# Delta rule inversion: 64x64 products paired across quarters of the array, four steps in place of five

## The chip, the cores and the metric

The kernel runs on one core of a Trainium2 chip. The metric is the device time of one execution in microseconds (us). A core has a matrix engine (TensorE, PE in the profile, with its weight loads listed as PEld), a vector engine (VectorE, DVE), a scalar engine (ScalarE, ACT), GpSimd (POOL) and SyncE (SP), which issues most DMAs. Each engine works through its own instructions in order and waits for others on semaphores. TensorE writes to PSUM; a PSUM tile must be read out (evacuated) by another engine before its buffer can be written again.

## The reference, cut to what matters

The program is one step of a two-layer encoder: a gated DeltaNet layer, then a layer of sliding-window attention. It works on 2048 prompt tokens and 32 sample tokens, with 8 heads of width 128. The delta rule is evaluated in blocks. For each block and head a lower triangular matrix with ones on its diagonal is built from the keys, and two right-hand sides are solved with it:

```python
lower = jnp.where(strict, jnp.einsum('nbhik,nbhjk->nbhij', kbeta, kc) * decay, 0.0)
tmat = lower + jnp.eye(c, dtype=lower.dtype)
u = lax.linalg.triangular_solve(tmat, vc * bc[..., None], left_side=True, lower=True, unit_diagonal=True)
...
def step(s, xs):
    v_new = ui - jnp.einsum('bhck,bhkv->bhcv', wi, s)
    o = jnp.einsum('bhck,bhkv->bhcv', qd, s) + jnp.einsum('bhij,bhjv->bhiv', ai, v_new)
    s = s * gl[..., None, None] + jnp.einsum('bhck,bhcv->bhkv', kd, v_new)
```

The state `s` goes from block to block, so the blocks follow one another.

## The kernel before

The kernel has stages. First come the projections of the DeltaNet layer with its convolution (class `P1`), then the delta rule (class `Delta`), then the layer's output projection with its norm (`O1`), the projections of the second layer (`P2`) and the attention (`Attention`). All products are in 32-bit floats, and one product appears in the profile as two passes of weight load and matmul.

The delta rule takes 17 chunks: the 32 sample tokens, and 16 chunks of 128 prompt tokens. The 16 big chunks need an inverse of a 128x128 unit triangular matrix for each of 8 heads. It is built up in sizes. The inverses of the 32x32 diagonal blocks come from an elimination on GpSimd and VectorE (`chain`, L546), and are transposed into place on VectorE and ScalarE (`spread`, L622, with the results `tcf` and `u32`). The method `invert` (L637) combines them on TensorE, for all 8 heads at a time. It is a generator: each `yield` ends a step, and the loop in `run` decides by its order of `next` calls what stands between the steps. `npr` holds the matrix, `u` the transposed inverse, and "lo" and "hi" below are rows or columns 0-63 and 64-127. The steps are:

1. `y1p` (L653): 32x32 products; ScalarE writes them, negated, into `y1` (L655).
2. `tp` (L659): 8 products from rows lo to columns lo; ScalarE copies them to `ta` lo (L661).
3. `up` (L666): 16 products, for each head one lo to lo and one hi to hi; two copies into `u` (L667, L668).
4. `y2p` (L672): 8 products, rows lo to columns hi; a copy to `ta` hi (L673).
5. `u2p` (L677): 8 products, rows hi to columns lo; ScalarE writes them, negated, into `u` (L678).

The PSUM tiles come from pools: `pa` (two buffers, shared with the transposes `tr` and `vtr` and the products `g` and `gq` of neighbouring chunks) and `pb` (one buffer). The steps use `pb`, `pa`, `pb`, `pa`, `pb`, in this order.

`run` (L775) works on several chunks at once. In pass `i` it finishes the recurrence for chunk `i`, inverts for chunk `i+1`, prepares chunk `i+2` and loads for chunk `i+3`. The orders of TensorE, VectorE and ScalarE are those of the program text (a manual schedule), so an instruction that waits holds back all that stands behind it on its engine. In one pass the calls around the inversion are, in order: step 1; step 2 among small VectorE operations; the transpose of keys `tr` (`turn_k`, L569) with its evacuation into `kd` by ScalarE (L572); steps 3 and 4; the transpose of values `vtr` (L583) with its evacuation into `vn` (L588); the exponentials `gb` (L611); the first product of `seen` (L712); the second `tr` and `kd`; the decays `E` (L518); step 5. The next pass begins with `lower` (L522) for another chunk, whose two groups of products `g` (L533) are read by VectorE into `npr` (L534). Then comes `changes` (L691): the products `vp` (L698) of `u` and `vn`, copied to `vs` by ScalarE (L700). From `vs` follow the outputs, the new state on VectorE (L734) and the next `errors` (`ks`, L687).

Between these, a `Filler` puts independent projection products (L77 to L79, tile `ps`) into TensorE's order in the first eleven passes, in fixed amounts; at the end products of the output projection (L1089 to L1091, tile `po`) take their place.

## Time and profile before

| | |
|---|---|
| median of 3 runs | 2277.91 us (2274.84 to 2278.19) |
| span of the profiled execution | 2272.4 us |
| TensorE (PE) busy | 2192.9 us (97%) |
| VectorE (DVE) busy | 1376.3 us (61%) |
| ScalarE (ACT) busy | 898.1 us (40%) |
| GpSimd (POOL) busy | 829.3 us (36%) |
| first step 1 to last step 5 of the inversions | 761.2 to 1183.6 us |

The profiled execution's own time is not listed beside its span; the span runs from its first to its last instruction, and lies 2.4 to 5.8 us below the runs' times, which take in what is around it. A row in order of time has the start and the length in us, the engine, the line, the operation, the tile written and the tiles read, the shapes, and a count of merged instructions; in brackets stand the idle time of the engine before it and what ended it. A row by line has counts and durations in ns, and below it who waited, as us and times. PE spans are modelled and overlap, since matmuls are pipelined. PEclk is the granted TensorE clock in tenths of full speed.

### The profile page before, as it was taken

The page shows a single profiled execution, that of the slowest core. Times are in us where ns is not written, and L with a number is a line of the kernel's source. Part 1 is how long each engine was busy: PE and PEld are TensorE (multiplying, and loading weights), DVE is VectorE, ACT ScalarE, POOL GpSimd, SP SyncE. Part 2 cuts the span into 40 slices and gives each one's busy share as a digit, 9 for nine tenths or more (in the row PEclk, how much of TensorE's full clock was granted, in tenths as well). Part 3 has the DMA queues.
Part 4 walks back from the last instruction along what each step waited for, and adds up shares of the span by engine and source line. Part 5 has one row for each costly group of instructions (what it writes and reads, how often), then busy time and mean ns, then how long its engine had stood idle before and what let it go on. Part 6 is the DMA issues. An engine that isn't in the chain of part 4 may idle for free.

```text
span 2272.4 us, 36806 instructions
## 1 busy us (share of the span) xinstructions
PE 2192.9 (97%) x13810; PEld 2008.0 (88%) x13810; DVE 1376.3 (61%) x2709; ACT 898.1 (40%) x2230; POOL 829.3 (36%) x1185
## 2 busy tenths in 40 slices
PE   8999999999998999999999999999999999999997
PEld 6999999999997888898888787999999987778884
DVE  3766666744385677777768875224443235668774
ACT  4444444333233566666642212311111235535541
POOL 1412121212120577766720201323442124556563
PEclk9999999999999999999889999999999999999998
DMA  5121212232435455557736764742212277233311
GB/s 191 66 77 66 75 66 80 103 108 103 126 114 144 93 129 130 120 125 186 189 91 196 227 192 149 252 146 70 73 68 77 83 179 249 75 94 96 109 61 51
DMA packets 282722, 274.49 MB, mean 121 GB/s; under 512 B 68608, under 2 KB 247104, under 8 KB 279200
## 3 DMA queue, kind: packets, MB, share of 16 engines
q1 hardware_dynamic: 270544, 248.84, 38.0%
q10 hardware_dynamic: 12000, 23.30, 2.9%
q8 instruction: 109, 1.79, 0.3%
q14 instruction: 69, 0.57, 0.1%
HBM read 168.53 MB, written 103.92 MB: 120 GB/s over the span
## 4 chain that ended last, share of the span: by engine, by line
PE 84%; ACT 6%; DMA 4%; DVE 3%; issue 1%; SPq 1%; POOL 0%; ACTq 0%; DVEq 0%; POOLq 0%
PE ps L77 16%; PE ps L79 16%; PE ps L78 16%; PE ot L1510 4%; PE po L1395 2%; PE po L1089 2%; PE po L1397 2%; PE po L1396 2%; PE po L1091 2%; PE po L1090 2%; PE S L1489 2%; PE tr L1504 2%; PE vp L698 2%; ACT kd L572 1%; DMA v<-s_v 1%
## 5 line engine op out<-in xcount | busy, mean ns | idle before, releaser
L77 PE MATMUL ps<-act_hi,w_hi 128*128 128x416 f32 x2000 | 707.9, 355 | 14.3 <-DVE z L266 7.9
L79 PE MATMUL ps<-act_hi,w_lo 128*128 128x416 f32 x2000 | 705.7, 353 | 2.8 <-DVE w_lo L54 1.8
L78 PE MATMUL ps<-act_lo,w_hi 128*128 128x416 f32 x2000 | 702.3, 351 | 0.0
L77 PEld LDWEIGHTS ps<-act_hi,w_hi 128*128 128x128 f32 x2000 | 377.6, 189 | 19.4 <-issue 8.6
L79 PEld LDWEIGHTS ps<-act_hi,w_lo 128*128 128x128 f32 x2000 | 376.5, 188 | 7.9 <-DVE w_lo L54 3.1
L78 PEld LDWEIGHTS ps<-act_lo,w_hi 128*128 128x128 f32 x2000 | 377.1, 189 | 4.5 <-DVE act_lo L69 0.2
L54 POOL TENSOR_TENSOR w_lo<-w_raw,w_hi 128x1024 fp32r<-128x1024 f32 x51 | 134.5, 2638 | 559.5 <-ACT w_hi L53 541.7
L196 DVE SCALAR_TENSOR_TENSOR y<-R,convw,y 128x2083 f32<-128x2083 f32 x72 | 173.7, 2414 | 110.1 <-POOL convo L190 56.9
L556 POOL TENSOR_TENSOR tm<-L,Tt 128x60 f32<-128x60 f32 (+19 forms) x373 | 140.0, 375 | 138.3 <-DVE tm L556 57.3
L1497 POOL TENSOR_TENSOR P<-P,sm 128x384 f32<-128x384 f32 (+2 forms) x128 | 100.5, 806 | 179.4 <-DVE sm L1374 104.3
L559 POOL TENSOR_TENSOR Tt<-Tt,tm 128x60 f32<-128x60 f32 (+19 forms) x373 | 151.7, 407 | 29.2
L1370 ACT ACTIVATE P<-S,nm 128x192 f32<-128x192 f32 (+2 forms) x260 | 104.7, 419 | 93.3 <-DVE nm L1363 40.4
L226 ACT COPY R<-ps 128x416 f32<-128x416 f32 (+1 forms) x144 | 61.2, 448 | 202.3 <-PE ps L79 177.7
L53 ACT CAST w_hi<-w_raw 128x1024 fp32r<-128x1024 f32 x62 | 65.0, 1048 | 146.2 <-PE ps L78 110.4
L1089 PE MATMUL po<-wo_hi,g_hi 128*128 128x512 f32 (+1 forms) x272 | 111.0, 408 | 2.9 <-ACT hT L1142 1.8
L1232 POOL TENSOR_TENSOR rs<-rs,sin 128x416 f32<-128x416 f32 x50 | 71.0, 1420 | 116.0 <-DVE rs L1231 102.1
L1091 PE MATMUL po<-wo_hi,g_lo 128*128 128x512 f32 (+1 forms) x272 | 107.3, 395 | 0.0
L1090 PE MATMUL po<-wo_lo,g_hi 128*128 128x512 f32 (+1 forms) x272 | 107.2, 394 | 0.0
L1510 PE MATMUL ot<-pt,vd 128*128 128x256 f32 x372 | 98.7, 392 | 2.1 <-ACT pt L1506 1.6
L1395 PE MATMUL po<-wo,g_hi 128*128 128x512 f32 x240 | 99.3, 414 | 0.0
L1397 PE MATMUL po<-wo,g_lo 128*128 128x512 f32 x240 | 96.2, 401 | 0.0
L1396 PE MATMUL po<-wo,g_hi 128*128 128x512 f32 x240 | 96.1, 400 | 0.0
(284 smaller groups left out, 4021.4 us busy)
## 6 DMA issues: line engine op xcount, KB each, us to landing
w_raw<-in_w_in SPq DMA_DIRECT2D x40, 512.0 KB
w_raw<-in_b_w_in SPq DMA_DIRECT2D x20, 512.0 KB
gb<-s_gcum SPq DMA_DIRECT2D x34, 256.0 KB
k<-s_k SPq DMA_DIRECT2D x34, 256.0 KB
s_z<-z SPq DMA_DIRECT2D x40, 208.0 KB
s_bz<-za SPq DMA_DIRECT2D x40, 208.0 KB
s_bq<-ra SPq DMA_DIRECT2D x40, 208.0 KB
s_q<-y SPq DMA_DIRECT2D x8, 1024.0 KB
```

The costliest lines, as they stand in the source:

```text
L77: nc.tensor.matmul(ps, hi[:, k, :], xh[:, k, :], start=(k == 0), stop=False)
L78: nc.tensor.matmul(ps, hi[:, k, :], xl[:, k, :], start=False, stop=False)
L79: nc.tensor.matmul(ps, lo[:, k, :], xh[:, k, :], start=False, stop=(k == KC - 1))
L196: nc.vector.scalar_tensor_tensor(out=y[:], in0=R[:, j:j + W], scalar=self.convw[:, i, j:j + 1], in1=y[:], op0=ALU.mult, op1=ALU.add)
L559: P.tensor_tensor(out=Tt[:n, i0:, :w], in0=Tt[:n, i0:, :w], in1=tm[:n, i0 - k:, :w], op=ALU.subtract)
L1089: nc.tensor.matmul(ps[:n], ghi[:, k, :n], w[0][:, k, cs], start=(k == 0), stop=False)
L1090: nc.tensor.matmul(ps[:n], ghi[:, k, :n], w[1][:, k, cs], start=False, stop=False)
L1091: nc.tensor.matmul(ps[:n], glo[:, k, :n], w[0][:, k, cs], start=False, stop=(k == KC - 1))
L1395: nc.tensor.matmul(ps[:n], ghi[:, k, :n], w[0][:, k, cs], start=(k == 0), stop=False)
L1396: nc.tensor.matmul(ps[:n], ghi[:, k, :n], w[1][:, k, cs], start=False, stop=False)
L1397: nc.tensor.matmul(ps[:n], glo[:, k, :n], w[0][:, k, cs], start=False, stop=(k == KC - 1))
L1510: nc.tensor.matmul(ot[:, p], self.vd[:, kc0 + j, p, :], pt[:, 2 * j:2 * j + 2, :], start=(j == 0), stop=(j == nj - 1))
```

## The change

Steps 2 to 4 become two. The product for `u` hi moves from step 3 up to step 2, and the product `y2p` moves from step 4 up to step 3. In the loops the two kinds of products alternate, so that neighbours use different quarters of the array. The copies on ScalarE move with them; their number stays. The last step's tile comes from `pa` instead of `pb`, by the alternation of the pools. `run` calls one step less after the side work.

```diff
+        lo, hi = halves
         tp = new(self.pa)
         for p in range(8):
-            nc.tensor.matmul(tp[:64, p, :], u32[:64, p, :], y1[:64, p, :], start=True, stop=True)
+            nc.tensor.matmul(tp[lo, p, :], u32[lo, p, :], y1[lo, p, :], start=True, stop=True)
+            nc.tensor.matmul(tp[hi, p, :], y1[hi, p, :], u32[hi, p, :], start=True, stop=True)
         ta = sml.tile([128, 8, 64], F32, tag="ta", name="ta")
-        nc.scalar.copy(ta[:64], tp[:64])
+        nc.scalar.copy(ta[lo], tp[lo])
+        nc.scalar.copy(u[hi, :, 64:128], tp[hi])
         yield
-        up = new(self.pb)
+        yp = new(self.pb)
         for p in range(8):
-            for hv in halves:
-                nc.tensor.matmul(up[hv, p, :], y1[hv, p, :], u32[hv, p, :], start=True, stop=True)
-        nc.scalar.copy(u[0:64, :, 0:64], up[0:64])
-        nc.scalar.copy(u[64:128, :, 64:128], up[64:128])
+            nc.tensor.matmul(yp[lo, p, :], y1[lo, p, :], u32[lo, p, :], start=True, stop=True)
+            nc.tensor.matmul(yp[hi, p, :], npr[lo, p, 64:128], ta[lo, p, :], start=True, stop=True)
+        nc.scalar.copy(ta[hi], yp[hi])
+        nc.scalar.copy(u[lo, :, 0:64], yp[lo])
         yield
-        y2p = new(self.pa)
+        u2p = new(self.pa)
         for p in range(8):
-            nc.tensor.matmul(y2p[64:128, p, :], npr[:64, p, 64:128], ta[:64, p, :], start=True, stop=True)
-        nc.scalar.copy(ta[64:128], y2p[64:128])
-        yield
-        u2p = new(self.pb)
-        for p in range(8):
-            nc.tensor.matmul(u2p[:64, p, :], ta[64:128, p, :], u[64:128, p, 64:128], start=True, stop=True)
-        nc.scalar.mul(u[:64, :, 64:128], u2p[:64], -1.0)
+            nc.tensor.matmul(u2p[lo, p, :], ta[hi, p, :], u[hi, p, 64:128], start=True, stop=True)
+        nc.scalar.mul(u[lo, :, 64:128], u2p[lo], -1.0)
         yield
...
-            go(v, r, v)
+            go(v, r)
```

Everything else in the program is unchanged; below `invert` the changed kernel's line numbers are lower by two.

## The prediction

> **What bounds the kernel now.** I read the page first, for the bound engine and the granted clock, then the view by line of the inversion's last product and its reader, and then the order in time around two inversions. I number the inversions 1 to 16; the first starts at 761 us, the last at 1169 us.

> ```profile
> span 2272.4 us, 36806 instructions
> PE 2192.9 (97%) x13810; PEld 2008.0 (88%) x13810; DVE 1376.3 (61%) x2709; ACT 898.1 (40%) x2230; POOL 829.3 (36%) x1185
> PEclk9999999999999999999889999999999999999998
> ```

> TensorE looks full and ScalarE idle, but that is the mean over the whole program. The stage of the change is one fifth of it, and there the readers of the last step's result tell another story:

> ```profile
> L678 ACT ACTIVATE u<-bps x16: 587/602/603, 772.8 to 1183.0; 64x512 f32<-64x512 f32 x16
>   PE vp L698: 6.9, 13
> ```

> In 13 of 16 inversions TensorE stands still before `vp`, waiting for ScalarE to write `u`. So I look at one inversion in order of time, number 3: TensorE first, then ScalarE.

> ```profile
> 817.88 1.14 PE L659 MATMUL bps<-y,u 64*64 64x64 f32 x16
> 818.95 0.66 PE L569 MATMUL tr<-ident,k 128*128 128x128 f32 x4
> 819.54 0.97 PE L666 MATMUL bps<-u,y 64*64 64x64 f32 x26
> 820.52 0.92 PE L672 MATMUL bps<-ta,npr 64*64 64x64 f32 x13
> 821.37 0.66 PE L583 MATMUL vtr<-ident,v 128*128 128x128 f32 x4
> 822.75 0.60 PE L569 MATMUL tr<-ident,k 128*128 128x128 f32 x4
> 823.28 1.14 PE L677 MATMUL bps<-u,ta 64*64 64x64 f32 x16
> 824.36 1.16 PE L533 MATMUL g<-k 128*128 128x128 f32 x8
> 825.67 1.16 PE L533 MATMUL g<-k 128*128 128x128 f32 x8 [0.15 <-ACT kd L572]
> 827.28 2.05 PE L698 MATMUL vp<-vn,u 128*128 128x128 f32 x16 [0.45 <-ACT u L678]
> ```

> ```profile
> 819.11 0.58 ACT L661 COPY ta<-bps 64x512 f32<-64x512 f32 x1 [2.56 <-PE bps L659]
> 819.64 1.14 ACT L572 ACTIVATE kd<-tr,t_ekd 128x128 f32<-128x128 f32 x4
> 820.73 0.58 ACT L667 COPY u<-bps 64x512 f32<-64x512 f32 x1
> 821.32 0.58 ACT L668 COPY u<-bps 64x512 f32<-64x512 f32 x1
> 821.81 0.58 ACT L673 COPY ta<-bps 64x512 f32<-64x512 f32 x1
> 822.41 1.14 ACT L588 ACTIVATE vn<-vtr,t_hn 128x128 f32<-128x128 f32 x4
> 824.47 1.15 ACT L572 ACTIVATE kd<-tr,t_ekd 128x128 f32<-128x128 f32 x4
> 826.63 0.60 ACT L678 ACTIVATE u<-bps 64x512 f32<-64x512 f32 x1
> ```

> From 819.11 to 827.23 ScalarE has no gap: it paces this stretch. TensorE delivers `u2p` by 824.42 (L677), and ScalarE reaches its evacuation (L678) 2.2 us later, being in order. `vp` starts 0.05 us after L678 ends, and everything of the recurrence (`vs`, state, next `ks`, next inversion) follows `vp`. Whatever moves `vp` moves the loop.

> **The change, part by part.** *TensorE products.* As before there are 40 64x64 products, each of two passes. The 16 L659 passes take 1.14 us; the paired L666 has 32 passes in about the same time. So the new first pair (`tp`, 32 passes) ends where L659 ended; its cost is nothing. Of the second pair (`yp`), one product reads rows 0-63 into columns 0-63 and the other rows 0-63 into columns 64-127. The nearest rows are those of inversion 2, where L672 (the latter quarter) began while L666 was still running:

> ```profile
> 793.74 0.27 PE L672 MATMUL bps<-ta,npr 64*64 64x64 f32 x1
> 793.78 0.28 PE L666 MATMUL bps<-u,y 64*64 64x64 f32 x3
> 793.85 0.22 PE L672 MATMUL bps<-ta,npr 64*64 64x64 f32 x1
> 793.85 0.27 PE L666 MATMUL bps<-u,y 64*64 64x64 f32 x2
> 793.90 0.22 PE L672 MATMUL bps<-ta,npr 64*64 64x64 f32 x1
> ```

> Three quarters advance at once, so I take `yp` at L666's time (the other end: twice that, 0.9 us later). TensorE is then free about 0.75 us earlier, since L672's tail is gone. I count none of that as a gain: what comes next on TensorE ends at waits for ScalarE, below. [...]

> *ScalarE.* The same five evacuations stand in another order: the copy to the lower-right `u` moves from behind `kd` (L668) to before it, and one evacuation fewer stands between `kd` and `vn`. In inversion 3, `kd` followed `ta` without a gap, so the moved copy pushes `kd` by 0.58 us and the rest comes out even: gain 0. Where ScalarE waited for the transpose `tr` instead, the copy fits in the hole:

> ```profile
> 791.76 0.58 ACT L661 COPY ta<-bps 64x512 f32<-64x512 f32 x1 [1.50 <-PE bps L659]
> 793.09 1.14 ACT L572 ACTIVATE kd<-tr,t_ekd 128x128 f32<-128x128 f32 x4 [0.75 <-PE tr L569]
> 1060.49 1.14 ACT L572 ACTIVATE kd<-tr,t_ekd 128x128 f32<-128x128 f32 x4 [0.41 <-PE tr L569]
> 1065.16 1.09 PE L583 MATMUL vtr<-ident,v 128*128 128x128 f32 x4 [1.46 <-DMA v<-s_v]
> 1119.66 1.09 PE L583 MATMUL vtr<-ident,v 128*128 128x128 f32 x4 [0.97 <-DMA v<-s_v]
> ```

> There the 0.75 us hole hides the copy, and `vn`, the second `kd`, `E` and L678 come 0.55 us earlier. In inversions 12 and 14 `vn` waits for the load of `v` instead, so nothing is gained.

> *PSUM.* This edit I weigh most. One `pa` tile moved: `u2p` was in `pb` and is now in `pa`, whose two buffers rotate. In the built program the order in `pa` becomes `tp`, `tr`, `vtr`, `tr`, `u2p`, `g`, `g`. So `u2p` must wait for `vn` (L588), the first `g` for the second `kd`, and the second `g` for the evacuation of `u2p`, which is L678. `vp` then has no wait of its own: `g` has taken it. Before, the second `g` ran at 825.67, under ScalarE's work; now it starts where `vp` did, at 827.28, and `vp` stands behind it. Its price: 16 passes of `vp` take 2.05 us with a last pass of 0.275 us, so a pass is (2.05 - 0.275)/15 = 0.118 us, and the 8 passes of `g` take 0.95 us. The waits of `u2p` (823.6 instead of 823.28) and of the first `g` (825.67 instead of 824.36) cost nothing while L678 is later; VectorE's read of `g` waits for `E` as it did.

> *DMA and POOL.* No transfer is added or moved, nor any POOL instruction. DVE, in order, takes the shift from `vp` through `otr`. I cost these at nothing; the cover is that they start from the same events.

> *The sum.* Inversions with no hole: 1, 3, 5, 7, 9, 10, at +0.95, is 5.7. With the hole: 2, 4, 6, 8, 11 at 0.95 - 0.55 = +0.4, is 2.0, and 13 (a hole of 0.41 us) the same, 0.4; the five are the row behind this paragraph, where `tr` waited for `ta`, 0.7 us each. Inversions 12 and 14: 2 x 0.95 = 1.9. Inversion 15 has no `g` behind it and gains 0.5; in 16 TensorE's own filling products stand between, 0. Together +9.5 us.

> ```profile
>   PE tr L569: 3.6, 5
> ```

> *The clock.* In inversion 3 TensorE would stand still from about 822.6 to 823.6 (before `u2p`), from 824.7 to 825.67 (before `g`) and from 826.6 to 827.28 (before the second `g`), 2.6 us in 4.7 us. Does that lower the granted clock? Nearest stretches, 3.41 us each (columns: length, busy PE, PEld, DVE, ACT, POOL, clock, DMA):

> ```profile
> 1033.73:1037.14 3.41, 2.69 (x56) 2.33 (x54) 3.24 (x11) 2.43 (x7) 2.94 (x7) 1.00 1.01 279
> 1054.21:1057.62 3.41, 1.93 (x42) 1.66 (x42) 3.27 (x9) 1.66 (x4) 2.71 (x10) 1.00 0.75 132
> 1057.62:1061.04 3.42, 3.42 (x32) 2.97 (x34) 1.55 (x7) 1.13 (x4) 2.71 (x10) 0.50 0.62 116
> 1081.51:1084.93 3.42, 2.06 (x44) 1.76 (x43) 3.18 (x10) 0.91 (x2) 2.73 (x9) 1.00 0.72 102
> 1084.93:1088.34 3.41, 3.41 (x25) 3.07 (x24) 2.57 (x10) 0.75 (x2) 2.77 (x9) 0.50 0.79 271
> ```

> After stretches with 1.93 and 2.06 us of PE the clock went to 0.50; after 2.69 it did not. A new stall that fills such a stretch would do the same, and half clock for 3.41 us loses at most 1.7 us. Bounds: 14 x 1.7 = +24 if every stall falls so, and about -8 if the four old drops (inversions 12 to 15, some 2 us each by the length of the products in them) were all missed by the shift. I estimate three new ones and one or two old ones gone: +1. [...]

> The sum is +10.5 us, on a span of 2272.4 us. The runs took 2274.84 to 2278.19 us (median 2277.91), so 2 to 6 us lie around the span; I add the shift to the median: 2288 us.

> **The rivals.** *TensorE is the bound, and its freed time counts* (the other side): 0.75 us in each of 15 inversions, -11 us, 2267 us. It decides from the point at which L678 would run before the first `g` has ended; in inversion 3 L678 ends at 827.23, 1.7 us after the first `g` did. For it: 97% busy; against it: the idle rows before `vp`. *The wait is absorbed*: some later wait that isn't in the loop, a load or the filling projections, swallows 0.95 us; then only the holes' gains and losses are left, 2278 us. Against it: TensorE and VectorE both take up the shift. *A pair doesn't run side by side*: if it is the second, `ta` comes 0.9 us later where ScalarE has the hole (6 x 0.9) and 0.3 us where it hasn't (8 x 0.3), +8 more, 2296 us; if it is the first too, 16 x 0.9 on top, 2310 us. The L672 and L666 rows speak against it. *The clock falls in most of the new stalls*: eight of 14 at 1.7, 2299 us.

> **How the numbers follow.** Forecast 0.55; clock in most stalls 0.17; absorbed 0.13; TensorE bound 0.09; unpaired 0.06. The measurement tells about 0.2% (4.6 us) from no change. Slower 0.55 + 0.17 + 0.06 = 0.78, same 0.13, faster 0.09. The range, 2279 to 2302, leaves out the TensorE case, half of the absorbed one and the clock's tail, some 0.18.

> **What would show it.** The idle time "until ACT u" moves from `vp` to L533, some 0.5 us each; from the first pair's start to `vp`, inversion 3 goes from 9.40 to about 10.35 us, and by 0.55 us less where there is a hole; both pairs last about 1.15 us; the copies stay at 0.58 us; drops of the clock around `vp`. I am wrong if `vp` starts 0.05 us after the evacuation of `u2p`, or if the loop from `vp` to the next `tcp` gets shorter.

## The result, and the profile after

The changed kernel takes 2302.85 us (median of four runs, 2299.27 to 2311.71), the kernel before in the same job 2276.38 us: a ratio of 1.0121, 95% interval 1.0098 to 1.0144. A second job gave 2297.14 us (five runs) against 2276.11 us, ratio 1.0104 (1.0087 to 1.0121). So the change costs 21 to 26 us where +10.5 us was forecast; the first median lies just above the range, the second inside it. The kernel before, run a second time as if it were a change, had a ratio of 0.9997 (0.9975 to 1.0019).

The page of the changed kernel, its span, TensorE's row and the row of the granted clock:

```profile
span 2299.8 us, 36806 instructions
PE 2187.4 (95%) x13810; PEld 2002.3 (87%) x13810; DVE 1375.1 (60%) x2709; ACT 899.2 (39%) x2230; POOL 831.8 (36%) x1185
PEclk9999999999999999999899999999999999999998
```

The sums moved by less than 6 us on every engine. The 27.4 us are not work, and the page can't show where they went. The view of the changed kernel by the line of the last evacuation, with those who waited for it (us, times), can:

```profile
L676 ACT ACTIVATE u<-bps x16: 587/604/608, 771.1 to 1203.8; 64x512 f32<-64x512 f32 x16
  PE g L533: 4.2, 10
```

Before, `vp` stood in this place. Now the products `g` wait for `u`. Inversion 3 in order of time, TensorE first and then ScalarE, in the changed kernel:

```profile
819.73 0.66 PE L569 MATMUL tr<-ident,k 128*128 128x128 f32 x4
...
821.60 0.66 PE L583 MATMUL vtr<-ident,v 128*128 128x128 f32 x4
...
822.99 0.60 PE L569 MATMUL tr<-ident,k 128*128 128x128 f32 x4
824.52 1.14 PE L675 MATMUL bps<-u,ta 64*64 64x64 f32 x16 [0.93 <-ACT vn L588]
826.57 1.16 PE L533 MATMUL g<-k 128*128 128x128 f32 x8 [0.91 <-ACT kd L572]
828.22 1.16 PE L533 MATMUL g<-k 128*128 128x128 f32 x8 [0.49 <-ACT u L676]
829.21 1.95 PE L696 MATMUL vp<-vn,u 128*128 128x128 f32 x16
```

```profile
819.90 0.58 ACT L663 COPY ta<-bps 64x512 f32<-64x512 f32 x1 [2.58 <-PE bps L661]
820.50 0.58 ACT L664 COPY u<-bps 64x512 f32<-64x512 f32 x1
821.11 1.14 ACT L572 ACTIVATE kd<-tr,t_ekd 128x128 f32<-128x128 f32 x4
822.27 0.58 ACT L670 COPY ta<-bps 64x512 f32<-64x512 f32 x1
822.86 0.58 ACT L671 COPY u<-bps 64x512 f32<-64x512 f32 x1
823.34 1.12 ACT L588 ACTIVATE vn<-vtr,t_hn 128x128 f32<-128x128 f32 x4
825.39 1.12 ACT L572 ACTIVATE kd<-tr,t_ekd 128x128 f32<-128x128 f32 x4
827.56 0.61 ACT L676 ACTIVATE u<-bps 64x512 f32<-64x512 f32 x1
```

All three waits of the rotation are there. `u2p` (L675) waits for `vn`, the first `g` for `kd`, the second `g` for `u`, and `vp` has no wait of its own. It starts 1.65 us after the evacuation of `u` does (829.21 - 827.56); before it was 0.65 us. In the table below, each profile is cut at the starts of the 1st and the 11th step 1 and of the 16th `vp`; "wait for v" is the idle time of the transposes `vtr` (L583) before the load of `v`, and "half clock" the time at a granted clock of about 0.50 in the first ten passes:

| us | before | after | after, second job |
|---|---|---|---|
| start to 1st step 1 | 761.2 | 759.4 | 761.4 |
| ten passes, 1st to 11th step 1 | 269.3 | 283.9 | 285.2 |
| 11th step 1 to 16th `vp` | 153.9 | 161.9 | 162.0 |
| 16th `vp` to the end | 1087.9 | 1094.6 | 1091.5 |
| half clock in the ten passes | 0 | 20.5 | 23.9 |
| wait for `v`, 1020 to 1210 us | 2.4 | 13.6 | 12.9 |

Of the +27.4 us of the first profile, +14.6 arose in the ten passes, +8.0 in the last six inversions, +6.7 in the later stages, and -1.8 ahead of the first inversion. The later stages run the same instructions in both kernels. In the profiles of the experiments they took 1080.5 to 1090.6 us, whatever the inversion was; the changed kernel's two values lie 1 to 4 us above all of these, and that part stays unexplained.

### The profile page after: what moved, and what is told of

It is laid out like the page before. It is cut to its first block, busy times and chain, and to the rows that moved or that the text cites. A ratio compares the mean times of both kernels' runs of the same rounds, so it can differ in the third digit from the quotient of the medians.

```text
span 2299.8 us, 36806 instructions
## 1 busy us (share of the span) xinstructions
PE 2187.4 (95%) x13810; PEld 2002.3 (87%) x13810; DVE 1375.1 (60%) x2709; ACT 899.2 (39%) x2230; POOL 831.8 (36%) x1185
## 4 chain that ended last, share of the span: by engine, by line
PE 84%; ACT 6%; DMA 4%; DVE 4%; issue 1%; SPq 1%; POOL 0%; ACTq 0%; DVEq 0%; POOLq 0%
PE ps L77 16%; PE ps L79 16%; PE ps L78 16%; PE ot L1508 4%; PE po L1087 2%; PE po L1089 2%; PE po L1088 2%; PE po L1393 2%; PE po L1395 2%; PE po L1394 2%; PE S L1487 2%; DMA v<-s_v 2%; PE tr L1502 2%; PE vp L696 2%; PE g L533 1%
```

## The experiments

**The rotation, taken away and done alone.** First the changed kernel with its last product back in `pb`, then the kernel before with nothing but that product in `pa`.

```diff
 # after, with u2p in pb
-        u2p = new(self.pa)
+        u2p = new(self.pb)
 # before, with u2p in pa
-        u2p = new(self.pb)
+        u2p = new(self.pa)
```

> The changed kernel with one line back: the tile of the last step (u2p) comes from pb again, so the two products g no longer wait for its evacuation; the pairs and the order of the copies stay. Theory of the rotation (the moved tile costs all of it, directly and by the clock): vp starts 0.05 us after u's evacuation again, 9.3 to 9.6 us after the first pair's start in inversions 1 to 11, no half clock between 780 and 1040 us, and 2266 to 2278 us in all, no slower than the kernel before. Rival, that the pairs or the order of the copies cost it: still 2295 us or more.

> The kernel before with only the tile of the last step taken from pa in place of pb; five steps, nothing paired anew. Theory of the rotation: the second g waits for u's evacuation, vp is 1.0 us later in every inversion from 1 to 14, without the 0.55 us that the moved copy gives where ScalarE has a hole; with new drops of the clock 2295 to 2310 us. Rival, that pairs and copies cost it: 2272 to 2282 us, as the kernel before.

Measured: with `u2p` in `pb` 2275.58 us (10 runs), ratio 0.999 (0.9969 to 1.001); the rotation alone 2291.4 us (10 runs), ratio 1.0069 (1.0041 to 1.0097). In the time of a run, one word of the diff makes the whole loss, to within the interval of some 2 us, and makes most of it in the kernel before too (a little less than expected). The rotation alone takes 283.9 us for the ten passes, as long as the changed kernel does, with 13.7 us at half clock. TensorE in inversion 3 of the changed kernel with `u2p` in `pb`:

```profile
823.40 1.14 PE L675 MATMUL bps<-u,ta 64*64 64x64 f32 x16
824.47 1.16 PE L533 MATMUL g<-k 128*128 128x128 f32 x8
826.46 1.16 PE L533 MATMUL g<-k 128*128 128x128 f32 x8 [0.83 <-ACT kd L572]
828.11 2.05 PE L696 MATMUL vp<-vn,u 128*128 128x128 f32 x16 [0.49 <-ACT u L676]
```

Both `g` are done under ScalarE's work, and `vp` alone waits for `u`. The ten passes take 268.0 us, 1.3 us less than before the change: what the merged steps are worth without the rotation. The last six inversions are another matter: with `u2p` in `pb` they still take 158.9 us, 5.0 us more than before the change, and the rotation adds 3.0 to that (161.9). In this profile the later stages took 1080.5 us, the least of all, which hides it; by the run times this kernel is at most some 2 us slower than the one before, so what the 5.0 us are worth over all runs is open.

**Work in the stall.** The changed kernel with four products of 128x128 (eight passes) more behind those of `u2p`, into a tile that nothing reads. They need no result of ScalarE that is late, and fill the wait before the first `g`.

```diff
+        idle = self.pb.tile([128, 4, 128], F32, tag="tr", name="idle")
+        for p in range(4):
+            nc.tensor.matmul(idle[:, p, :], self.G["ident"][:, :], npr[:, p, :], start=True, stop=True)
```

> The changed kernel with four more 128x128 products (8 passes, result not read) behind the last step's products, in the standstill ahead of g. They lengthen nothing if TensorE only waits there. Theory of the clock (standstills drop it, and the drops are a part of the loss of their own): no half clock between 780 and 1040 us, 10.5 us from the first pair to vp in inversions 1 to 11 alike, 2285 to 2293 us. Rival, that the drops come from elsewhere or cost nothing: the same drops or the same 2300 to 2305 us. If the products were in the way: more than 2305 us.

Measured: 2288.47 us (10 runs), ratio 1.0063 (1.0043 to 1.0083). More work makes the changed kernel 9 to 14 us faster. Its profile has no half clock in the ten passes, which take 276.9 us against 283.9. In passes of the changed kernel without a drop the two kernels agree (the first pass 27.55 and 27.57 us, the third 28.19 and 28.21), so the products cost nothing there. So 7.0 us of the loss in the ten passes were the clock; the other 276.9 - 269.3 = 7.6 us are the wait, 8.9 (276.9 - 268.0), less the 1.3 that the merged steps gain. In the last six inversions the products don't help: 164.7 us against 161.9. The view by stretches (columns: length, busy PE with its count, granted clock, DMA share, GB/s) shows how the clock falls, first in the changed kernel and then with the products in the stall. Each pair of rows is a stretch with the stall and the one after it:

```profile
795.09:798.50 3.41, 2.05 (x24) 1.00 0.55 150
798.50:801.91 3.41, 3.15 (x16) 0.51 0.02 5
825.81:829.22 3.41, 2.16 (x17) 1.00 0.02 7
829.22:832.63 3.41, 3.17 (x29) 1.00 0.00 0
...
880.42:883.83 3.41, 1.78 (x22) 1.00 0.55 154
883.83:887.25 3.42, 3.21 (x15) 0.51 0.00 0
```

```profile
823.73:827.14 3.41, 2.47 (x29) 1.00 0.40 112
827.14:830.55 3.41, 2.94 (x31) 1.00 0.21 62
936.37:939.78 3.41, 2.47 (x29) 1.00 0.58 152
939.78:943.19 3.41, 2.92 (x24) 1.00 0.02 6
```

At 2.05 us of TensorE in 3.41 us, the next 3.41 us ran at half clock, at 2.16 us (inversion 3) they didn't, and the eight passes lift the emptiest stretch to 2.47 us. What the low clock costs is seen in inversion 2 of the changed kernel, where the second `g` of 1.16 us takes 2.07:

```profile
797.75 1.39 PE L533 MATMUL g<-k 128*128 128x128 f32 x8 [0.91 <-ACT kd L572]
799.40 2.07 PE L533 MATMUL g<-k 128*128 128x128 f32 x8 [0.26 <-ACT u L676]
```

**The pairs pulled apart.** The changed kernel with `u2p` in `pb`, and the two products of each merged step in loops of their own, so that neighbours use the same quarter.

```diff
         for p in range(8):
             nc.tensor.matmul(tp[lo, p, :], u32[lo, p, :], y1[lo, p, :], start=True, stop=True)
+        for p in range(8):
             nc.tensor.matmul(tp[hi, p, :], y1[hi, p, :], u32[hi, p, :], start=True, stop=True)
...
         for p in range(8):
             nc.tensor.matmul(yp[lo, p, :], y1[lo, p, :], u32[lo, p, :], start=True, stop=True)
+        for p in range(8):
             nc.tensor.matmul(yp[hi, p, :], npr[lo, p, 64:128], ta[lo, p, :], start=True, stop=True)
```

> As e1_u2p_in_pb, but in both merged steps the eight products of one kind stand ahead of the eight of the other, so that neighbours use the same quarter. Theory that pairs run side by side and that this is worth their length: the first copy comes as before (its products stand first), the copy of u hi and the second copy of ta come 0.9 us later each where ScalarE isn't already behind; from the first step to vp 0.3 to 1.0 us more than in e1_u2p_in_pb, 5 to 14 us in all. Rival, that the hardware overlaps them in any order, or that the time is hidden: within 3 us of e1_u2p_in_pb.

Measured: 2282.89 us (10 runs), ratio 1.0035 (1.0015 to 1.0056), and 275.1 us for the ten passes against 268.0 paired. The interleaving is worth 0.71 us a pass; without it the four steps would be slower than the five. The 32 passes of a pair take 1.90 us pulled apart; paired, 1.15 us for the first pair and 1.15 to 1.36 for the second. In the changed kernel the second pair does run side by side (TensorE, inversion 3):

```profile
820.64 0.22 PE L669 MATMUL bps<-ta,npr 64*64 64x64 f32 x1
820.64 0.22 PE L668 MATMUL bps<-u,y 64*64 64x64 f32 x1
820.69 0.22 PE L669 MATMUL bps<-ta,npr 64*64 64x64 f32 x1
820.70 0.22 PE L668 MATMUL bps<-u,y 64*64 64x64 f32 x1
```

**The last evacuation ahead of the decays.** On ScalarE the decays `E` (L518) stand before the evacuation of `u2p`. Three kernels move the last step of the inversion ahead of them: the changed one with `u2p` in `pb`, the changed one as it is, and the one before.

```diff
-            go(w, r, p, r, seen, k, r, d, r)
+            go(w, r, p, r, seen, k, r, v, d, r)
...
-            go(v, o, d)
+            go(o, d)
```

> As e1_u2p_in_pb, and the last step is called ahead of the first half of the decays E, so that ScalarE evacuates u2p right behind kd, about 1.15 us sooner. Theory that ScalarE's order paces vp: from the first pair to vp 8.7 us in place of 9.6 in inversions 1 to 10 (then the second g, which waits for kd, is the last thing ahead of vp), some 0.9 us in each of 14 inversions, 2260 to 2268 us. Rival, that the wait only moves to E and its readers: within 3 us of e1_u2p_in_pb, 2272 to 2279 us.

> The changed kernel (u2p in pa), with the last step called ahead of the first half of E as in e5_pb_early_evacuation. Theory of the rotation: the second g still waits for u's evacuation, and that is 1.15 us sooner, so from the first pair to vp 9.4 us in place of 10.56, with shorter standstills and fewer drops of the clock: 2275 to 2286 us. If the place of the evacuation doesn't pace it: 2297 us or more.

> The kernel before, five steps, with the last step called ahead of the first half of E. If the pairing and the saved step are worth something once the wait is gone, this is slower than e5_pb_early_evacuation: from the first product to vp 8.8 us where ScalarE has no hole and 9.1 where it has, 2262 to 2270 us. If they are worth nothing: within 1 us of e5_pb_early_evacuation.

Measured, in this order: 2274.4 us (12 runs), ratio 0.9995 (0.998 to 1.001); 2286.54 us (8 runs), 1.005 (1.0031 to 1.0069); 2270.14 us (12 runs), 0.9974 (0.9957 to 0.9991). The ten passes take 262.0, 272.1 and 263.3 us, so the edit is worth about 6 us there without the rotation (268.0 and 269.3 before it) and 11.8 us with it. But with `u2p` in `pb` the last six inversions go from 158.9 to 165.1 us and take it back, while in the kernel before they fall to 149.3 us. So the first of the three missed its expectation and matches the rival in time (though not in the ten passes), and the second lies just above the range of its own. The third, five steps and an earlier evacuation, is the fastest of them, where its expectation had it slower than the first if the pairing is worth something; its ScalarE in inversion 3:

```profile
823.91 0.60 ACT L678 ACTIVATE u<-bps 64x512 f32<-64x512 f32 x1
824.39 2.46 ACT L518 ACTIVATE E<-E,t_ngc 128x128 f32<-128x128 f32 x8
```

Products into an unread tile at the start of `invert`, for the late chunks alone, were added to it to see whether the clock drops there could be bought off too:

```diff
+        if ch.t0 >= 1408:
+            idle = self.pb.tile([128, 4, 128], F32, tag="tr", name="idle")
+            for p in range(4):
+                nc.tensor.matmul(idle[:, p, :], self.G["ident"][:, :], npr[:, p, :], start=True, stop=True)
```

> As e7_before_early_evacuation, and in inversions 12 to 16 four 128x128 products (result not read) stand ahead of the first step, where TensorE waits about 1 us for tcp. Theory of the clock: fewer half-clock stretches between 1040 and 1180 us than the 20 to 50 us of the other profiles, and 2262 to 2269 us. Rival, that the load of v sets the pace there: the same stretches or the same time, 2268 to 2272 us.

Measured: 2269.37 us (11 runs), ratio 0.9982 (0.9967 to 0.9997), no better; half clock in the last six inversions 23.9 us against 20.5, and the stretch 154.5 us against 149.3. Whether the products were too few or at the wrong place was not tried.

**Where the last six inversions lose.** There the transposes `vtr` wait for the load of `v`. The view of waits, TensorE from 1020 to 1210 us (us in total, times, longest), of the kernel before, the changed kernel, and the changed one with `u2p` in `pb`:

```profile
PE vtr L583 <- DMA v<-s_v: 2.4, 2, 1.5
```

```profile
PE vtr L583 <- DMA v<-s_v: 13.6, 4, 6.1
```

```profile
PE vtr L583 <- DMA v<-s_v: 12.8, 3, 5.2
```

The length of this wait is not what it costs: the kernel before with the earlier evacuation waits 7.7 us there and has the shortest stretch (149.3 us), and the one with the pairs pulled apart waits 3.3 us and takes 159.8. A first try gave this load a buffer more, and took it from the loads of `q`, in both kernels:

```diff
-                    t = self.four.tile([128, 4, w], F32, tag="q", name="q", bufs=5)[:]
+                    t = self.four.tile([128, 4, w], F32, tag="q", name="q", bufs=4)[:]
-                    t = self.sml.tile([128, 4, w], F32, tag="vz", name=name, bufs=3)[:]
+                    t = self.sml.tile([128, 4, w], F32, tag="vz", name=name, bufs=4)[:]
```

> The changed kernel with four buffers for the loads of v and z (three before) and four for those of q (five before), so that the load of v for inversion 12 to 14 need no longer wait until a buffer of this rotation is read. If the 8.0 us that the change loses from the 11th to the 16th inversion are the waits of vtr for that load (13.6 us against 2.4), the waits fall below 4 us, the stretch from the 11th y1 to the last vp goes from 162.0 to about 155 us, and the time lies some 6 us below the changed kernel, near 2292 to 2296 us, with the first ten passes at about 284 us as they were. Rival: the load is late because the transfers share the DMA engines with the weights that come in there; then its issue moves earlier, the waits stay above 8 us, and the stretch stays within 2 us of 162. Second rival: the waits go but the stretch stays, because something else (drops of the clock, the order on ScalarE) takes their place.

> The kernel before with the same edit. By the first theory it has 2.4 us of these waits to lose: the stretch from the 11th y1 to the last vp goes from 154.0 to 152 to 154 us and the time stays within 3 us of 2276; the difference between the two kernels in this stretch falls from 8.0 to about 2 us. By the rivals the stretch is 154 and the difference stays at about 8. If the fourth q buffer missing costs anything, it shows in both as a wait for q, and in the first ten passes (269.3 us without the edit).

Measured: 2365.95 us and 2367.11 us (4 runs each), both at a ratio of 1.039. The wait for `v` is gone, but the buffer taken from `q` costs far more (TensorE from 760 to 1300 us, changed kernel and kernel before):

```profile
PE gq L602 <- DMA q<-s_q: 62.8, 13, 11.0
```

```profile
PE gq L602 <- DMA q<-s_q: 62.0, 13, 11.2
```

That says nothing of the question, and both times miss what was expected. Where passes wait for a load, the difference between the two kernels is gone, as far as four runs that scatter by 10 us can tell.

The second try takes the load of `v` away from the five last chunks; `vtr` reads the keys in its place, so these kernels leave out the values of those chunks.

```diff
+            if name == "v" and ch.t0 >= 1408:
+                ch.__dict__.setdefault("v", []).append(ch.k[:, hs, :])
+                continue
```

> The changed kernel without the load of v for the last five chunks, whose transposes vtr read the keys k in its place, which are there a pass earlier (so the values of these chunks are not used; all instructions of the engines stay, ten DMAs of 256 KB go). If the waits for v are what the change loses from the 11th inversion on, this kernel and the kernel before with the same edit differ in the stretch from the 11th y1 to the last vp by about the terms forecast for it, 2 to 3 us, and not by 8.0; the stretch itself falls from 162 to about 152 to 155 us, and the time to about 2290 to 2294 us. By the rival (the clock or the order on ScalarE) the difference in the stretch stays near 8 us.

> The kernel before with the same edit: it has 2.4 to 4.6 us of these waits to lose, so the stretch from the 11th y1 to the last vp goes from 154 to 150 to 153 us and the time is 1 to 4 us below 2276. By the rival the same, with the changed kernel 8 us above it.

> The changed kernel with u2p in pb and without the late loads of v. With u2p in pb the stretch took 158.9 us, 5 us over the kernel before, at 12.8 us of waits for v. If these are its loss, the stretch comes to that of the kernel before with the same edit or 1 us below it (the pass is 0.13 us shorter in the first ten), and the time lies at 2268 to 2273 us; by the rival it stays 5 us above.

Measured: 2293.61 us (4 runs), ratio 1.0067 (1.0046 to 1.0087); 2268.84 us (6 runs), 0.996 (0.9945 to 0.9976); 2269.83 us (9 runs), 0.9971 (0.9957 to 0.9985). The stretch from the 11th step 1 to the 16th `vp` is 156.0, 152.7 and 152.0 us. The changed kernel falls by 5.9 us, the kernel before by 1.2, the one with `u2p` in `pb` by 6.9. The two kernels now differ by 3.3 us in this stretch instead of 8.0, so 4.7 us of the difference hang on the load of `v`. That fits the 5.0 us that stayed with `u2p` in `pb`: without the load, that kernel is no longer slower there than the one before. All three came as expected but for the first one's stretch (1 us more) and the second one's time (7 us below the kernel before, where 1 to 4 were expected). It is one profile each, and not a clean cut: some of the time comes back as waits of `g` for the load of the keys (4.7 us in the changed kernel, 6.3 us in the one before).

The two kernels as they are were run again, in one job with the kernel that has products for the late chunks:

> The changed kernel once more, unaltered, for a second profile and more times. What belongs to it comes again: 283 to 285 us from the first to the eleventh inversion with about 20 us at half clock, against 269 us before; what was chance in the first profile (some 7 us in the stages behind the delta rule) doesn't. 2296 to 2306 us.

> The kernel before once more, for a second profile beside the first: how far the stretch of inversions 11 to 16 (153.9 us in the first) and the stages behind it (1088 us) differ from one execution to the next. If the waits for the load of v (2.4 us in the first profile, 13 us in four-step kernels) are chance, they come out anywhere from 2 to 14 us here; if they belong to four steps, 2 to 8 us again.

Their times stand in the result. The parts of the loss came again: 285.2 against 269.3 us in the ten passes, 162.0 against 154.0 us behind them. The kernel before waited 4.6 us for `v` this time (2.4 in its first profile), the changed one 12.9 (13.6).

## Why the prediction was right or wrong

| part, us | forecast | measured | by |
|---|---|---|---|
| the wait, ten passes | +9.5 | +8.9 | 276.9 - 268.0 |
| the order on ScalarE, ten passes | -2.2 | -1.3 | 268.0 - 269.3 |
| the clock, ten passes | +1 in all | +7.0 | 283.9 - 276.9 |
| inversions 11 to 16 | +2.2 | +8.0 | 161.9 - 153.9 |
| later stages | 0 | +6.7, second job +4.1 | 1094.6 - 1087.9, 1091.5 - 1087.4 of the kernel before run again |

The first two terms are right in kind, and their sum (+7.3 forecast, +7.6 measured) is closer than they are, because their errors cancel: that part is luck.

*TensorE products: right.* Both pairs run side by side, the second at times 0.2 us longer than the pace taken for it. Pulled apart they cost 0.71 us a pass, about half of what I had priced for both (8 + 16 x 0.9 us over 16 inversions, 1.4 each). The freed time of TensorE gained nothing that shows, as said: the 1.3 us in ten passes with `u2p` in `pb` are those of the order on ScalarE, four passes with a hole shorter by about 0.6 us and six without longer by about 0.18. The two products of the first pair write the two row halves of one tile (`tp`) and ran side by side: 1.15 us for their 32 passes against 1.90 pulled apart.

*ScalarE: right but for 0.16 us.* From the first pair to the last evacuation the passes without a hole went from 8.75 to 8.91 us, where I said 0: the same four copies and `kd` take 3.44 us up to `vn` in the new order (819.90 to 823.34), and took 3.30 us in the old one (819.11 to 822.41). The hole was filled as said: 9.54 became 8.91 to 8.97 us.

*PSUM: right.* This was the part that I weighed most, and the part that decides. The wait is 1.0 us (0.65 to 1.65), against 0.95 from the length of eight passes. From the first pair to `vp`, inversion 3 went from 9.40 to 10.56 us (forecast 10.35), and inversion 8, which has the hole, from 10.20 to 10.60 us (forecast 10.60).

*The clock: the term that failed.* The prediction took "three new ones and one or two old ones gone: +1". There were six new ones in the ten passes, seven in the second job. The old ones lie behind these passes, and none clearly went: from the 11th step 1 to the 16th `vp` half clock took 41.0 and 34.1 us in the two profiles of the kernel before, 34.1 and 37.5 us in those of the changed one. So the term came to +7.0 us where it had +1. The cause was named and the figures were on record; the count was a guess, and the figures spoke for more than three. Before, half clock followed 2.06 us of work in 3.41 us and did not follow 2.69, and the forecast stalls (822.6 to 823.6, 824.7 to 825.67, 826.6 to 827.28) take at least 1.3 us from every stretch of 3.41 us that starts between about 821.6 and 825.0. That is as long as the stretch itself, so if such stretches are laid end to end, each such pass would hold one with 2.1 us or less, wherever they begin. That the clock goes by them was an estimate from the few rows of before. The 2.1 us are just above the row that dropped (2.06), so those rows left open how many would: in the end six or seven of ten. The rival "the clock falls in most of the new stalls" (2299 us, a chance of 0.17) is what happened in the ten passes, at 7.0 / 6 = 1.2 us a drop where it had 1.7 as the most; another profile with the same first ten passes (the changed kernel without the late loads) had eight drops and took 287.1 us. That its total is near the measured one is partly luck: it had 13.6 us for the clock and nothing for the load of `v` or the later stages. By its own terms it comes to 2301 us (2277.91 + 9.5 + 8 x 1.7), and the "absorbed" case, with only the gains of the holes and of inversion 15 left, to some 2274; neither changes the forecast.

*Inversions 12 to 14: the other miss.* I saw the waits for `v` there and concluded only that nothing is gained. In inversion 12 of the changed kernel (TensorE, in order of time) the wait was 4.94 us where it had been 1.46:

```profile
1080.23 1.09 PE L583 MATMUL vtr<-ident,v 128*128 128x128 f32 x4 [4.94 <-DMA v<-s_v]
```

Step 1 of this inversion starts at 1069.93 us, in the kernel before at 1055.20. So `vtr` has its load 10.3 us after it, and had it 10.0 us after it before, while TensorE comes to `vtr` 5.4 us after step 1 (1080.23 - 4.94 - 1069.93), where it took 8.5 (1065.16 - 1.46 - 1055.20). Most of that difference is not the saved step. In the kernel before, TensorE ran at half clock from 1057.62 us on, 6.1 of the 8.5 us; at full clock, without the late loads, five steps come to `vtr` after 5.8 us and four after 5.3. So the wait grew because no low clock covered it any more, and `vp` can't come before the load in either kernel. What four steps make earlier there is lost to the load, the load itself comes later after step 1 (0.3 us in inversion 12, 11.4 against 9.5 us in inversion 14), and the wait of the rotation comes on top. Without the load the two kernels differ by 3.3 us in the stretch, near the 2.2 forecast. The load itself took 11.4 us from its issue (1068.84) to `vtr`, before 9.7 us (1055.51 to 1065.16); why it takes longer, and whether the loads of weights in this stretch slow it, was not tried.

*DMA and POOL* were costed at nothing, which the load of `v` contradicts: no transfer was added, but the cover of one was thin, and the text should have named what it costs when gone. The later stages' +4 to +7 us stay open.

*The rivals.* TensorE as the bound fell: less work on TensorE's path gained nothing that shows in the ten passes, and more work gained 9 to 14 us in all. "Absorbed" is false for this kernel, but the two kernels with four buffers for `q`, 1.2 us apart, are what it may look like.

## What to carry to other kernels

A tile that moves into a pool of rotating buffers can bring its reader's delay to the unrelated tiles behind it in the rotation, as `u2p` did to `g` and `vp` (8.9 us in the ten passes); before moving one, write down who evacuates it, when, and who takes the buffer next. Short stalls had a second price here, 7.0 us in the ten passes: half clock followed six stretches of 3.41 us with 1.78 to 2.16 us of TensorE. Slide a stretch of that length over the stall pattern of a pass, see how much work is left in the emptiest position, and compare it with what stood before the drops in a trace of the kernel; if it is too little, work that nobody needs can pay for itself, as it did in the ten passes here (276.9 us against 283.9), but not in the last six inversions (164.7 against 161.9). And a step made faster in the middle of a pipeline should be checked against the loads that were only just in time; what such a wait costs is read from the length of the pass, not from the length of the wait.

## What the runs showed of the hardware

Two 64x64 products that read the same rows of their operands and write different halves of the tile ran side by side (L668 and L669 above, one of each starting every 0.05 to 0.06 us; 1.15 to 1.36 us for 32 passes), as did two that share neither (L660 and L661, one of each every 0.05 to 0.06 us in inversion 3; 1.15 us for 32 passes).

One thing was not foreseen on ScalarE: moving one evacuation ahead of the 2.46 us of decays, an edit of the order alone, is worth more in the ten passes (6.0 us in the kernel before) than the whole regrouping of the products without the rotation (1.3 us).
